# Seven products of quarters for the gate and up blocks of a two-block layer

## The chip, the cores and the metric

The kernel runs on one core of one Trainium2 chip. The metric is device microseconds of one execution. Before the change three executions took 1948.46, 1948.71 and 1949.76 us; the median is 1948.71 us. One further execution was profiled: 1947.45 us, of which the span from its first to its last instruction is 1945.6 us.

## The reference, cut to what matters

The program computes two transformer blocks in float32 on 512 tokens of width 1024 (the second block puts 16 meta tokens in front). The change touches the two feed-forward layers of the second block:

```python
def swiglu(u, w_gate, w_up, w_down):
    return (jax.nn.silu(u @ w_gate) * (u @ w_up)) @ w_down
...
h = h + 0.5 * swiglu(rmsnorm_2(h, ffn1_norm[l]), ffn1_w_gate[l], ffn1_w_up[l], ffn1_w_down[l])
h = h + hybrid_mixer(...)
h = h + 0.5 * swiglu(rmsnorm_2(h, ffn2_norm[l]), ffn2_w_gate[l], ffn2_w_up[l], ffn2_w_down[l])
y = rmsnorm_2(h, final_norm)
return y[:, N_META:]
```

`w_gate` and `w_up` are 1024 x 2816, `w_down` is 2816 x 1024.

## The kernel before, in words

Activations lie transposed: 1024 features are 8 blocks (k = 0 to 7) of 128 partitions, tokens run along the free axis. The first feed-forward layer (FFN1) works on all n = 528 tokens, the second (FFN2) on n = 512. Every float32 operand is split into a high part, rounded to the matmul's type, and a low part, the rest; `mm3` (L233) makes a product as three matmuls: weights high by x high (L235), weights high by x low (L236), weights low by x high (L237). The split inputs are `xhi` and `xlo`.

A list of jobs (L1468, L1489) gives the order of the weight loads. `_dma` (L179) issues one from SyncE's queue into a raw tile `wraw` of which there are two. `_conv` (L186) converts four k blocks at a time, called a chunk here: ScalarE copies the raw weights to `whi` (L198), VectorE subtracts to get `wlo` (L199), each 128x512. There are five buffers of each, so a chunk is converted when the product that used the chunk five before it has ended. `w` (L219) hands the converted weights to a product.

`ffn` (L896) runs twice over one half of the 22 blocks of 128 columns of gate and up, and then the down product of that half. For each of the 11 blocks f of a half it makes the gate product (8 k blocks, three matmuls each; in FFN1 each in two parts of 264 columns, in FFN2 in one of 512), multiplies it by the row of inverse norms `r` (L933, VectorE), applies SiLU (L934, ScalarE), makes the up product, multiplies by `r` (L939) and by g (L940), and splits the result into `ahi` (L941, ScalarE) and `alo` (L942, VectorE). One gate block and the up block of the same f are called a pair below; there are 22 in each layer. The down product adds half of its result to the running `hT` (L952). In the last layer the last two down blocks are made in halves of 256 tokens (L963, L965), with the final norm behind each half (L311 to L1462).

No order is written out by hand below the code's own: the tile framework orders each engine's instructions when the program is built, and sets the waits between engines.

Of the kernel before, what the change touches and what calls it, by code (L numbers as in the profile page):

```python
# [17 lines left out]
KB = 8  # L18
# [3 lines left out]
XW = 576  # L22
EPS = 1e-6
# [143 lines left out]
class Net:  # L167
# [5 lines left out]
    def jobs(self, jobs):  # L173
        self.joblist = jobs
        self.j_dma = self.j_conv = self.k_conv = self.j_use = self.n_conv = self.n_use = 0
        self.raws, self.convd = {}, {}
        self.kept = 0

    def _dma(self, j):  # L179
        src, i, k0, nk = self.joblist[j]  # L180
        ncol = src.shape[3]
        t = self.wpool.tile([128, nk, ncol], F32, name="wraw", tag="wraw", bufs=self.RAWB)
        self.nc.sync.dma_start(t, src[i, :, k0:k0 + nk, :])
        self.raws[j] = t

    def _conv(self):  # L186

        j, k = self.j_conv, self.k_conv
        raw = self.raws[j]
        nk, ncol = raw.shape[1:]  # L190
        n = min(self.CK, nk - k)
        if j < len(self.joblist) - self.kept:
            pool, x, b = self.wpool, "w", self.CONVB
        else:
            pool, x, b = self.kpool, "k", 2 * self.kept
        hi, lo = (pool.tile([128, n, ncol], F32R, name=x + y, tag=x + y, bufs=b) for y in ("hi", "lo"))
        x = raw[:, k:k + n, :]
        self.nc.scalar.copy(hi, x)  # L198
        self.nc.vector.tensor_sub(lo, x, hi.bitcast(F32))  # L199
        his, los = self.convd.setdefault(j, ([], []))  # L200
        his += [hi[:, i, :] for i in range(n)]
        los += [lo[:, i, :] for i in range(n)]
        self.n_conv += 1
        self.k_conv += n
        if self.k_conv == nk:
            self.raws.pop(j)
            self.j_conv, self.k_conv = j + 1, 0
# [19 lines left out]

    def convert(self, free=0):

        while self.j_conv < len(self.joblist) and self.n_conv < self.n_use + free + self.CONVB:  # L230
            self._conv()

    def mm3(self, ps, whi, wlo, xhi, xlo, start, stop):  # L233
        mm = self.nc.tensor.matmul
        mm(ps, whi, xhi, start=start, stop=False)  # L235
        mm(ps, whi, xlo, start=False, stop=False)  # L236
        mm(ps, wlo, xhi, start=False, stop=stop)  # L237
# [658 lines left out]
    def ffn(self, t0, done, split=KB, half_done=None):  # L896

        nc, tc = self.nc, self.tc  # L900
        V, A, P = nc.vector, nc.scalar, nc.tensor
        n = T - t0
        parts = [(0, 264), (264, n - 264)] if n > 512 else [(0, n)]
        aw = n if n <= 512 else XW
        self.open_psum()
        with tc.tile_pool(name="ff", bufs=1) as pool:
# [7 lines left out]
            def product(p, hi, lo, x, k0, k1, first, last):  # L914
                for k in range(k0, k1):
                    for c, w in parts:
                        self.mm3(p[:, c:c + w], hi[k - k0], lo[k - k0], *x(k, c, c + w),
                                 first and k == k0, last and k == k1 - 1)

            xs = lambda k, u, v: self.x(k, t0 + u, t0 + v)  # L920
            pool.tile([128, 40 if n > 512 else 64], F32, name="pad")
            ahi = pool.tile([128, 11, aw], F32R, name="ahi")
            alo = pool.tile([128, 11, aw], F32R, name="alo")
            as_ = lambda k, u, v: (ahi[:, k, u:v], alo[:, k, u:v])
            for half in range(2):
                for f in range(11):
# [3 lines left out]
                    if half == 0 and f == 0:  # L930
                        self.rstd([self.psc() for _ in range(2 if n > 512 else 1)], t0)
                    g = pool.tile([128, n], F32, name="g", tag="g", bufs=2)
# [5 lines left out]
                    u = pool.tile([128, n], F32, name="u", tag="u", bufs=2)  # L938
                    V.tensor_mul(u, p, r)  # L939
                    V.tensor_mul(u, u, g)  # L940
                    A.copy(ahi[:, f, 0:n], u)  # L941
                    V.tensor_sub(alo[:, f, 0:n], u, ahi[:, f, 0:n].bitcast(F32))  # L942
                for m in range(split if half else KB):
                    p = psum()
                    hi, lo = self.w()
                    product(p, hi, lo, as_, 0, 6, True, False)
                    hi, lo = self.w()
                    product(p, hi, lo, as_, 6, 11, False, True)
                    h = self.hT[:, m, t0:T]
                    if half and m == 0:  # L950
                        self.x0 = XW - T
                    V.scalar_tensor_tensor(h, p, 0.5, h, op0=OP.mult, op1=OP.add)  # L952
                    if half:
                        done(m, slice(t0, T))
            if split < KB:
                ws = [[x + y for x, y in zip(self.w(), self.w())] for m in range(split, KB)]
                for c in (slice(0, n // 2), slice(n // 2, n)):
                    x = slice(t0 + c.start, t0 + c.stop)
                    for m in range(split, KB):
                        hi, lo = ws[m - split]  # L960
                        p = psum()[:, 0:n // 2]
                        for k in range(11):
                            self.mm3(p, hi[k], lo[k], ahi[:, k, c], alo[:, k, c], k == 0, k == 10)  # L963
                        h = self.hT[:, m, x]
                        V.scalar_tensor_tensor(h, p, 0.5, h, op0=OP.mult, op1=OP.add)  # L965
                        done(m, x)
                    half_done(x, self.psc())

# [457 lines left out]
    def final(self, out):  # L1426
# [3 lines left out]
        with tc.tile_pool(name="fin", bufs=1) as pool:  # L1430
            hg = pool.tile([128, KB, T], F32, name="hg")
            ss, late = self.ssq, pool.tile([128, T], F32, name="sq7")
            rc = pool.tile([128, S // 2], F32, name="rcol")
            pool.tile([128, 24], F32, name="padk")
            self.kept, self.kpool = 4, pool

            def done(m, x):
                h = self.hT[:, m, x]
                if m == 0:
# [8 lines left out]
                A.activation(hg[:, m, x], h, AF.Copy, scale=self.gain[4][:, m:m + 1])  # L1448

            def half_done(x, p):  # L1450
                p = p[:, 0:S // 2]
                self.inv_rms([p], S // 2, [ss[:, x], late[:, x]], D)
                A.copy(rc, p)
                for m in range(KB):
                    o = hg[:, m, x]
# [4 lines left out]
                    if m % 2 == 0 or m == KB - 1:  # L1460
                        k = max(m - 1, 0) if m % 2 == 0 else m
                        (nc.scalar if m % 4 == 2 else nc.sync).dma_start(  # L1462
                            out[:, k:m + 1, x.start - NM:x.stop - NM], hg[:, k:m + 1, x])
# [25 lines left out]
def ffn_jobs(a, n):  # L1489
    j = []  # L1490
    for half in range(2):
        for f in range(11 * half, 11 * half + 11):
            j += [(a[n + "_gate"], f, 0, KB), (a[n + "_up"], f, 0, KB)]
# [31 lines left out]
```

## Time and profile before

| what | value |
|---|---|
| median of three executions | 1948.71 us |
| profiled execution | 1947.45 us |
| its span, first to last instruction | 1945.6 us |
| TensorE busy in matmuls | 1925.6 us, 99% of the span |
| VectorE busy | 1141.6 us, 59% |
| ScalarE busy | 796.4 us, 41% |
| GpSimd busy | 10.3 us, 1% |
| mean granted TensorE clock | 0.998 of full speed |
| bytes moved by DMA | 171.63 MB, 88 GB/s |

Times are microseconds unless marked ns. PE is TensorE with its matmuls, PEld its weight loads, DVE VectorE, ACT ScalarE, POOL GpSimd, SP SyncE. `L235` is line 235 of the kernel. Matmuls overlap one another, so how fast they go is read from the distance of their starts, not from their durations.

### The profile page before, as it was taken

To read this page: it belongs to the slowest core of one execution; us is meant where nothing else is said; L and a number is where in the kernel's file an instruction comes from. 1 tells how busy PE (TensorE), PEld (TensorE's weight loads), DVE (VectorE), ACT (ScalarE), POOL (GpSimd) and SP (SyncE) were. 2 spreads that over 40 slices of the span, in tenths; PEclk is the share of its full clock that TensorE was granted. 3 is DMA by queue.
4 is the path that set the end of the run, shared out by engine and by line. 5 is a ranking of instruction groups with operands and counts; after the bars stand their busy time and mean duration, and the time that the engine had idled before them with its cause. 6 is when DMAs were issued, how large, how long until landed. Compare 5 with 4: busy or idle time off the path is not lost.

```text
span 1945.6 us, 29528 instructions
## 1 busy us (share of the span) xinstructions
PE 1925.6 (99%) x11682; PEld 1691.6 (87%) x11682; DVE 1141.6 (59%) x2272; ACT 796.4 (41%) x1516; POOL 10.3 (1%) x31
## 2 busy tenths in 40 slices
PE   8999999999999999999999999999999999999998
PEld 6877788999999998889898898988888888888887
DVE  6789675444344458897554645877744554434443
ACT  7456654332233344453434333444433343323333
POOL 0010000000000000000000000000000000000000
PEclk9999999999999999999999999999999999999999
DMA  4352112222322242212122213111122222233223
GB/s 155 100 151 72 45 65 94 83 95 74 104 95 87 79 131 85 74 65 94 66 98 71 87 60 104 66 66 64 59 94 94 97 92 98 82 103 109 98 80 95
DMA packets 60682, 171.63 MB, mean 88 GB/s; under 512 B 10592, under 2 KB 13120, under 8 KB 60544
## 3 DMA queue, kind: packets, MB, share of 16 engines
q1 hardware_dynamic: 59456, 168.70, 26.3%
q8 instruction: 92, 1.51, 0.3%
q10 hardware_dynamic: 1088, 1.05, 0.2%
q14 instruction: 46, 0.38, 0.1%
HBM read 167.05 MB, written 2.67 MB: 87 GB/s over the span
## 4 chain that ended last, share of the span: by engine, by line
PE 93%; DVE 4%; ACT 1%; DMA 1%; issue 1%; SPq 0%; DVEq 0%; ACTq 0%
PE pm L235 27%; PE pm L236 27%; PE pm L237 27%; PE sc L235 2%; PE sc L236 1%; PE sc L237 1%; DVE rot L1036 1%; PE pf L752 1%; DVE wlo L199 1%; PE pn L784 0%; PE so L1301 0%; PE sc L1147 0%; DMA slot<-rd 0%; PE st L1131 0%; PE pd L472 0%
## 5 line engine op out<-in xcount | busy, mean ns | idle before, releaser
L235 PE MATMUL pm<-xhi,whi 128*128 128x264 f32 (+2 forms) x2360 | 787.6, 334 | 1.1 <-DVE hT L875 0.9
L236 PE MATMUL pm<-xlo,whi 128*128 128x264 f32 (+2 forms) x2360 | 781.5, 331 | 0.0
L237 PE MATMUL pm<-xhi,wlo 128*128 128x264 f32 (+2 forms) x2360 | 779.1, 330 | 0.0
L198 ACT CAST whi<-wraw 128x512 fp32r<-128x512 f32 (+1 forms) x628 | 372.2, 593 | 813.8 <-PE pm L236 758.3
L199 DVE TENSOR_TENSOR wlo<-wraw,whi 128x512 fp32r<-128x512 f32 (+1 forms) x628 | 409.8, 653 | 314.7 <-ACT whi L198 304.0
L235 PEld LDWEIGHTS pm<-xhi,whi 128*128 128x128 f32 (+1 forms) x2360 | 444.0, 188 | 46.3 <-issue 6.9
L237 PEld LDWEIGHTS pm<-xhi,wlo 128*128 128x128 f32 (+1 forms) x2360 | 444.2, 188 | 40.8 <-issue 1.7
L236 PEld LDWEIGHTS pm<-xlo,whi 128*128 128x128 f32 (+1 forms) x2360 | 443.6, 188 | 38.8 <-issue 1.2
L236 PE MATMUL pm<-alo,whi 128*128 128x264 f32 (+1 forms) x506 | 160.4, 317 | 0.0
L235 PE MATMUL pm<-ahi,whi 128*128 128x264 f32 (+1 forms) x506 | 159.6, 315 | 0.0
L237 PE MATMUL pm<-ahi,wlo 128*128 128x264 f32 (+1 forms) x506 | 159.6, 315 | 0.0
L237 PEld LDWEIGHTS pm<-ahi,wlo 128*128 128x128 f32 x506 | 95.4, 189 | 6.0
L235 PEld LDWEIGHTS pm<-ahi,whi 128*128 128x128 f32 x506 | 95.1, 188 | 6.0
L236 PEld LDWEIGHTS pm<-alo,whi 128*128 128x128 f32 x506 | 94.9, 187 | 6.0
L933 DVE TENSOR_TENSOR g<-pm,rT 128x528 f32<-128x528 f32 (+1 forms) x44 | 30.8, 700 | 73.7 <-PE pm L237 68.5
L939 DVE TENSOR_TENSOR u<-pm,rT 128x528 f32<-128x528 f32 (+1 forms) x44 | 30.8, 700 | 72.5 <-PE pm L237 72.5
L941 ACT CAST ahi<-u 128x528 fp32r<-128x528 f32 (+1 forms) x44 | 27.6, 627 | 63.9 <-DVE u L940 63.9
L235 PE MATMUL pm<-yhi,whi 128*128 128x512 f32 x128 | 49.8, 389 | 0.0
L236 PE MATMUL pm<-ylo,whi 128*128 128x512 f32 x128 | 49.8, 389 | 0.0
L237 PE MATMUL pm<-yhi,wlo 128*128 128x512 f32 x128 | 49.8, 389 | 0.0
L942 DVE TENSOR_TENSOR alo<-u,ahi 128x528 fp32r<-128x528 f32 (+1 forms) x44 | 30.8, 701 | 30.5 <-ACT ahi L941 30.5
L1036 DVE TENSOR_TENSOR rot<-pm,rope 32x384 f32<-32x384 f32 (+3 forms) x50 | 32.5, 650 | 0.7
(414 smaller groups left out, 2268.4 us busy)
## 6 DMA issues: line engine op xcount, KB each, us to landing
wraw<-in_w_in SPq DMA_DIRECT2D x124, 512.0 KB, 3.2
wraw<-in_ffn_gate SPq DMA_DIRECT2D x44, 512.0 KB, 3.2
wraw<-in_ffn_up SPq DMA_DIRECT2D x44, 512.0 KB, 3.2
wraw<-in_ffn_down SPq DMA_DIRECT2D x32, 384.0 KB, 3.0
wraw<-in_ffn_down SPq DMA_DIRECT2D x32, 320.0 KB, 2.8
wraw<-in_w_ret_out SPq DMA_DIRECT2D x32, 256.0 KB, 2.4
slot<-rd SPq DMA_DIRECT2D x4, 1024.0 KB, 9.4
wraw<-in_w_out SPq DMA_DIRECT2D x8, 512.0 KB, 3.2
```

The costliest lines, as they stand in the source:

```text
L198: self.nc.scalar.copy(hi, x)
L199: self.nc.vector.tensor_sub(lo, x, hi.bitcast(F32))
L235: mm(ps, whi, xhi, start=start, stop=False)
L236: mm(ps, whi, xlo, start=False, stop=False)
L237: mm(ps, wlo, xhi, start=False, stop=stop)
L752: P.matmul(p[:, 0:n], q[part, n - 128:n], dk[h][part, 0:n], start=True, stop=True)
L933: V.tensor_mul(g, p, r)
L939: V.tensor_mul(u, p, r)
L941: A.copy(ahi[:, f, 0:n], u)
L942: V.tensor_sub(alo[:, f, 0:n], u, ahi[:, f, 0:n].bitcast(F32))
L1036: V.tensor_mul(tmp[o:o + half], p[i:i + half], tab[i:i + half, 1, t:T])
```

## The change

The first four pairs of each layer stay as they were. The other 18 (36 of the 44 in all) are made by Strassen's scheme (Winograd's form of it): with the input cut into quarters by k (0 to 3, 4 to 7) and by tokens (first and second half, h = 264 or 256), and the weights into gate and up by k, seven products of quarters take the place of eight. Each product has 4 k blocks of three matmuls on h columns. Four combinations of the inputs' quarters (`thi`, `tlo`) are made once in a layer, by the generator `sums`, which is advanced between the products of the plain pairs. Four sums of weights are needed in each pair: `s1` (up, both halves of k) and `s3` (up and gate, first half) by loading one operand and then adding the other with a transfer that accumulates, issued from GpSimd's queue; `s2`, twice, by additions on VectorE. Seven chunks are converted in a pair in place of four. The partial results pass through PSUM: `px` and `py` go on accumulating after ScalarE has copied an intermediate state out of them (`c1`, `c5`, `c2`). The multiplication of up by `r` moves behind the down product (`rh`, 0.5 times r), which takes two VectorE instructions in place of one. In the last layer, the output tile and the kept weights move into tiles of the feed-forward pool.

The diff, cut to its core:

```diff
+PLAIN = 4
+    def _dma_pair(self, ga, ua, i):
+        nc = self.nc
+        lo, hi = slice(0, 4), slice(4, 8)
+        g, s, u = (self.fpool.tile([128, 8, 128], F32, name=x, tag="f4", bufs=6) for x in ("fg", "fs", "fu"))
+        s1, s3, u2, s2 = s[:, lo, :], s[:, hi, :], u[:, lo, :], u[:, hi, :]
+        nc.sync.dma_start(s1, ua[i, :, lo, :])
+        nc.sync.dma_start(g, ga[i])
+        nc.sync.dma_start(s3, ua[i, :, lo, :])
+        nc.sync.dma_start(u2, ua[i, :, hi, :])
+        nc.gpsimd.dma_start(s1, ua[i, :, hi, :], accum_op=OP.add)
+        nc.gpsimd.dma_start(s3, ga[i, :, lo, :], accum_op=OP.add)
+        return g, u2, s1, s3, s2
     def _conv(self):
+        if self.joblist[j][0] == "pair":
+            g, u2, s1, s3, s2 = raw
+            V = self.nc.vector
+            if k == 2:
+                V.tensor_add(s2, s1, g[:, 0:4, :])
+            elif k == 5:
+                V.tensor_add(s2, s2, g[:, 4:8, :])
+            x = (g[:, 0:4, :], s1, s2, g[:, 4:8, :], s3, s2, u2)[k]
+            self.chunkq.append(self._split(j, x))
...
     def prefetch(self, most=None):
-        while self.j_dma < min(n, self.j_conv + self.RAWB):
+        while self.j_dma < n:
+            if self.joblist[self.j_dma][0] == "pair":
+                if self.fpool is None or self.f_dma - self.f_done >= 2:
+                    return
+            elif self.p_dma - self.p_done >= self.RAWB:
+                return
+    def wq(self, last=False):
+        self.prefetch()
+        self.convert()
+        self.n_use += 1
+        self.j_use += last
+        return self.chunkq.pop(0)
     def ffn(self, t0, done, split=KB, half_done=None):
+            def sums():
+                hT, gc = self.hT, self.gain[1 if t0 == 0 else 3]
+                for k in range(4):
...
+                    for y, kk in ((y1, k), (y2, k + 4)):
+                        A.activation(y, hT[:, kk, t0:T], AF.Copy, scale=gc[:, kk:kk + 1])
+                    yield 1
...
+                    V.tensor_sub(q[:, 0], b11, b12)
+                    V.tensor_sub(q[:, 2], b22, b12)
+                    yield 1
+                    V.scalar_tensor_tensor(q[:, 1], q[:, 0], -1.0, b22, op0=OP.mult, op1=OP.subtract)
+                    V.scalar_tensor_tensor(q[:, 3], q[:, 1], -1.0, b21, op0=OP.mult, op1=OP.subtract)
+                    yield 1
+                    for u in (0, 2):
+                        A.copy(thi[:, u:u + 2, k, :], q[:, u:u + 2])
+                        V.tensor_sub(tlo[:, u:u + 2, k, :], q[:, u:u + 2], thi[:, u:u + 2, k, :].bitcast(F32))
+                        yield 1
+            def pair(f):
+                pm = self.pmain()
+                px, py, pz = pm[:, 0, 0:h], pm[:, 1, 0:h], self.psc()[:, 0:h]
...
+                def seven(p, x, first=False, last=False, end=False):
+                    whi, wlo = self.wq(end)
+                    for k in range(4):
+                        self.mm3(p, whi[k], wlo[k], *x(k), first and k == 0, last and k == 3,
+                                 skip_group_check=True)
...
+                seven(px, b11, first=True)
+                A.copy(c1, px)
+                seven(py, t(0), first=True)
+                A.copy(c5, py)
+                seven(px, t(1))
+                A.copy(c2, px)
+                seven(pz, b21, first=True, last=True)
+                V.tensor_add(g[:, 0:h], pz, c1)
+                seven(px, t(2))
+                V.tensor_add(u[:, h:n], px, c5)
+                seven(py, b22, last=True)
+                V.tensor_add(g[:, h:n], py, c2)
+                V.tensor_mul(g, g, r)
+                A.activation(g, g, AF.Silu)
+                seven(px, t(3), last=True, end=True)
+                V.scalar_tensor_tensor(u[:, h:n], u[:, h:n], -1.0, g[:, h:n], op0=OP.mult, op1=OP.mult)
+                V.scalar_tensor_tensor(u[:, 0:h], px, -1.0, g[:, 0:h], op0=OP.mult, op1=OP.mult)
+                gated(f % 11, u)
...
-                    V.scalar_tensor_tensor(h, p, 0.5, h, op0=OP.mult, op1=OP.add)
+                    y = temp("u")
+                    V.tensor_mul(y, p, rh)
+                    V.tensor_add(self.hT[:, m, t0:T], self.hT[:, m, t0:T], y)
...
-                        V.scalar_tensor_tensor(h, p, 0.5, h, op0=OP.mult, op1=OP.add)
+                        y = temp("u")[:, c]
+                        V.tensor_mul(y, p, rh[:, c])
+                        V.tensor_add(self.hT[:, m, x], self.hT[:, m, x], y)
```

In a pair the seven products are called p0 to p6 below, in the order of the code, and the chunk that each of them uses chunk 0 to chunk 6.

## Rows read from the trace of the kernel before

**Rows 1.** The page: span, TensorE's and VectorE's busy time, granted clock in 40 slices.
```profile
span 1945.6 us, 29528 instructions
...
PE 1925.6 (99%) x11682; PEld 1691.6 (87%) x11682; DVE 1141.6 (59%) x2272; ACT 796.4 (41%) x1516; POOL 10.3 (1%) x31
...
PEclk9999999999999999999999999999999999999999
```
**Rows 2.** Windows of one pair (FFN1, FFN2): length, engines' busy, clock, DMA share, GB/s.
```profile
377.38:389.06 11.68, 11.68 (x98) 11.68 (x97) 5.33 (x8) 3.77 (x7) 0.00 (x0) 1.00 0.25 87
1612.54:1623.42 10.88, 10.88 (x49) 9.01 (x48) 5.19 (x8) 3.74 (x7) 0.00 (x0) 1.00 0.29 101
```
**Rows 3.** Timeline of VectorE in a pair of FFN1: start, duration, instruction, idle before.
```profile
365.70 0.71 DVE L933 TENSOR_TENSOR g<-pm,rT 128x528 f32<-128x528 f32 x1 [1.64 <-PE pm L237]
...
371.54 0.71 DVE L939 TENSOR_TENSOR u<-pm,rT 128x528 f32<-128x528 f32 x1 [1.64 <-PE pm L237]
372.17 0.68 DVE L199 TENSOR_TENSOR wlo<-wraw,whi 128x512 fp32r<-128x512 f32 x1
372.77 0.70 DVE L940 TENSOR_TENSOR u<-u,g 128x528 f32<-128x528 f32 x1
...
377.38 0.71 DVE L933 TENSOR_TENSOR g<-pm,rT 128x528 f32<-128x528 f32 x1 [1.64 <-PE pm L237]
```
**Rows 4.** Timeline of VectorE in FFN2: the same instruction in two pairs that follow one another.
```profile
1612.54 0.69 DVE L933 TENSOR_TENSOR g<-pm,rT 128x512 f32<-128x512 f32 x1 [1.55 <-PE pm L237]
...
1623.42 0.69 DVE L933 TENSOR_TENSOR g<-pm,rT 128x512 f32<-128x512 f32 x1 [1.55 <-PE pm L237]
```
**Rows 5.** Timeline of TensorE at the end of FFN2: the first and the 34th 256-column matmul.
```profile
1918.34 0.28 PE L235 MATMUL pm<-ahi,khi 128*128 128x256 f32 x1
...
1922.29 0.28 PE L235 MATMUL pm<-ahi,khi 128*128 128x256 f32 x1
```
**Rows 6.** Groups of VectorE by line and form, FFN1: busy, mean ns of one, idle before.
```profile
L199 DVE TENSOR_TENSOR wlo<-wraw,whi 128x512 fp32r<-128x512 f32 x120 | 82.5, 687 | 77.4 <-ACT whi L198 75.1 <-PE pm L236 2.2
...
L940 DVE TENSOR_TENSOR u<-u,g 128x528 f32<-128x528 f32 x22 | 15.4, 701 | 0.0
```
**Rows 7.** The same for VectorE in FFN2: the 256-column forms.
```profile
L1459 DVE TENSOR_TENSOR hg<-hg,sc 128x256 f32<-128x256 f32 x12 | 4.2, 416 | 2.5 <-ACT rcol L1453 2.5
...
L965 DVE SCALAR_TENSOR_TENSOR hT<-pm,hT 128x256 f32<-128x256 f32 x4 | 1.7, 424 | 5.8 <-PE pm L237 5.8
```
**Rows 8.** The same for ScalarE in FFN1.
```profile
L198 ACT CAST whi<-wraw 128x512 fp32r<-128x512 f32 x121 | 75.2, 622 | 169.7 <-PE pm L236 167.4 <-DMA wraw<-in_ffn_down 1.6 <-ACT g L934 0.3
L934 ACT ACTIVATE g<-g 128x528 f32<-128x528 f32 x22 | 14.2, 648 | 4.2 <-DVE g L933 4.2
L941 ACT CAST ahi<-u 128x528 fp32r<-128x528 f32 x22 | 13.9, 633 | 31.1 <-DVE u L940 31.1
...
L289 ACT ACTIVATE xhi<-hT,par 128x528 fp32r<-128x528 f32 x8 | 5.9, 737 | 1.7 <-DVE hT L952 1.4 <-DVE hT L875 0.3
...
L325 ACT COPY rT<-sc 128x264 f32<-128x264 f32 x2 | 0.8, 380 | 2.1 <-PE sc L317 2.1
```
**Rows 9.** Timeline of ScalarE in the pair of rows 3.
```profile
365.62 0.62 ACT L198 CAST whi<-wraw 128x512 fp32r<-128x512 f32 x1 [2.29 <-PE pm L236]
366.44 0.65 ACT L934 ACTIVATE g<-g 128x528 f32<-128x528 f32 x1 [0.20 <-DVE g L933]
```
**Rows 10.** Timeline of the tail: the last down block's sum and the square behind it.
```profile
1935.80 0.42 DVE L965 SCALAR_TENSOR_TENSOR hT<-pm,hT 128x256 f32<-128x256 f32 x1 [2.44 <-PE pm L237]
1936.25 0.42 ACT L1447 ACTIVATE sq<-hT 128x256 f32<-128x256 f32 x1 [2.95 <-DVE hT L965]
```
**Rows 11.** DMA issues: transfer, queue, count, KB each, median us from issue to landing.
```profile
wraw<-in_ffn_gate SPq DMA_DIRECT2D x44, 512.0 KB, 3.2
...
wraw<-in_w_ret_out SPq DMA_DIRECT2D x32, 256.0 KB, 2.4
...
dfmask<-in_dfmask SPq DMA_DIRECT2D x1, 256.0 KB, 6.1
```

More of the change, by code (lines that the diff above doesn't have):

```diff
@@ new lines, in _split, with keep @@
+    def _split(self, j, x):
+        n, ncol = x.shape[1:]
+        if j < len(self.joblist) - self.kept:
+            hi, lo = (self.wpool.tile([128, n, ncol], F32R, name=y, tag=y, bufs=self.CONVB) for y in ("whi", "wlo"))
+        else:
+            hi, lo = self.keep(n)
+        self.nc.scalar.copy(hi, x)
+        self.nc.vector.tensor_sub(lo, x, hi.bitcast(F32))
+        return [hi[:, i, :] for i in range(n)], [lo[:, i, :] for i in range(n)]
+    def keep(self, n):
+        if self.kslot is None:
+            k = self.fpool.tile([128, 32, 128], F32R, name="khi", tag="tlo", bufs=1)
+            self.kslot = [(k, self.fpool.tile([128, 8, 128], F32R, name="klo", tag="f4", bufs=6), 8 * i)
+                          for i in range(4)]
+            self.kfree = 0
+        if self.kfree + n > 8:
+            self.kslot.pop(0)
+            self.kfree = 0
+        k, lo, o = self.kslot[0]
+        i = self.kfree
+        self.kfree += n
+        return k[:, o + i:o + i + n, :], lo[:, i:i + n, :]
@@ L189, in _conv @@
         raw = self.raws[j]
[L190 to L193, printed above, removed]
-        else:
[L195 to L202, printed above, removed]
+        if self.joblist[j][0] == "pair":
[7 more added lines that the diff above has]
+            self.chunkq.append(self._split(j, x))
+            k += 1
+            end = 7
+        else:
+            end = raw.shape[1]
+            n = min(self.CK, end - k)
+            hi, lo = self._split(j, raw[:, k:k + n, :])
+            his, los = self.convd.setdefault(j, ([], []))
+            his += hi
+            los += lo
+            k += n
         self.n_conv += 1
-        self.k_conv += n
-        if self.k_conv == nk:
+        self.k_conv = k
+        if k == end:
             self.raws.pop(j)
+            if self.joblist[j][0] == "pair":
+                self.f_done += 1
+            else:
+                self.p_done += 1
             self.j_conv, self.k_conv = j + 1, 0
@@ L927, in ffn @@
+            made = None
+            for half in range(2):
+                for f in range(11 * half, 11 * half + 11):
+                    if f >= PLAIN:
+                        if f == PLAIN:
+                            sides.drain(made)
+                        pair(f)
+                        continue
                     hi, lo = self.w()
@@ L929, in ffn @@
                     product(p, hi, lo, xs, 0, KB, True, True)
-                    if half == 0 and f == 0:
+                    if f == 0:
                         self.rstd([self.psc() for _ in range(2 if n > 512 else 1)], t0)
-                    g = pool.tile([128, n], F32, name="g", tag="g", bufs=2)
+                        V.tensor_scalar(rh, r, 0.5, None, op0=OP.mult)
+                        made = sides.add(sums())
+                    g, u = temp("g"), temp("u")
                     V.tensor_mul(g, p, r)
@@ L937, in ffn @@
                     product(p, hi, lo, xs, 0, KB, True, True)
[L938 to L942, printed above, removed]
+                    V.tensor_mul(u, p, g)
+                    gated(f, u)
                 for m in range(split if half else KB):
@@ L1430, in final @@
         with tc.tile_pool(name="fin", bufs=1) as pool:
-            hg = pool.tile([128, KB, T], F32, name="hg")
+            hgs = []
             ss, late = self.ssq, pool.tile([128, T], F32, name="sq7")
             rc = pool.tile([128, S // 2], F32, name="rcol")
-            pool.tile([128, 24], F32, name="padk")
-            self.kept, self.kpool = 4, pool
+            self.kept = 4
             def done(m, x):
+                if not hgs:
+                    hgs.append(self.fpool.tile([128, KB, S], F32, name="hg", tag="thi", bufs=1))
                 h = self.hT[:, m, x]
+                g = hgs[0][:, m, x.start - NM:x.stop - NM]
                 if m == 0:
@@ L1447, in done @@
                     A.activation(late[:, x], h, AF.Square)
[L1448 removed]
+                A.activation(g, h, AF.Copy, scale=self.gain[4][:, m:m + 1])
             def half_done(x, p):
```

73 lines of the change are left out of this document (52 added, 21 removed).

## The prediction

> **What bounds the kernel now.** I read the page first: TensorE is busy 99% of the span, VectorE 59%, and the granted clock stands at nine tenths or more of full speed in all 40 slices [rows 1]. Busy matmuls overlap, so this alone does not say that TensorE sets the pace. The windows of one pair in each layer do: TensorE has no idle time in either, VectorE is busy for 5.33 of 11.68 us and 5.19 of 10.88 us, ScalarE for 3.77 and 3.74, GpSimd not at all, and DMA uses 25 to 29% of its share [rows 2]. The same instruction comes back after exactly one such window: 11.68 us in FFN1 [rows 3], 10.88 us in FFN2 [rows 4]. Divided by the matmuls that the code puts into a pair, 2 x 8 x 2 x 3 = 96 of 264 columns and 2 x 8 x 3 = 48 of 512, that is 121.7 ns and 226.7 ns from start to start, with nothing lost where one product follows the other. What is worth reading here is therefore the number of matmuls times their step, as long as the other engines keep up.
>
> **Part 1, the matmuls of 36 pairs.** A pair becomes 7 x 4 x 3 = 84 matmuls. In FFN1 they have 264 columns as before: 84 x 121.7 ns = 10.22 us, 1.46 less than 11.68 [rows 3]; 18 pairs give 26.3 us. In FFN2 the columns are halved, so the weights change twice as often for the same columns, and the step of 512 does not halve. The end of the kernel already has 256-column matmuls of the same kind, 33 steps in 3.95 us, 119.7 ns [rows 5]: 84 x 119.7 ns = 10.05 us, 0.83 less than 10.88 [rows 4]; 18 pairs give 14.9 us. Together 41.2 us less.
>
> Here a rule can be weighed. The rows give 119.7, 121.7 and 226.7 ns for 256, 264 and 512 columns. The Trainium skill (TensorE: Matmul & The Clock Gate, "Back-to-back issue gap") gives columns / 2.4 + 2.5 ns at the full clock, an estimate of 109, 112.5 and 216 ns; by it a pair would gain 1.35 us in FFN1 and 1.19 us in FFN2, 45.7 us in all. The rows are 9 to 11 ns longer at every width, which weighs more on the narrow matmuls, and they decide.
>
> **Part 2, VectorE and ScalarE beside them.** VectorE in a pair of FFN1: seven subtractions for `wlo` and two additions for `s2`, nine of 128x512 at 0.687 us [rows 6] = 6.2 us; three additions and two products on 264 columns at 0.42 us, by the 256-column rows [rows 7] = 2.1; two on 528 columns (g by r, `alo`) at 0.70 [rows 6] = 1.4. The sum of durations is 9.7 us. But instructions that are ready run into each other: the one at 372.17 is followed 0.60 us later though it lasts 0.68 [rows 3]. With 0.09 us of overlap on each of the 16 the engine needs 8.3 us. Either is under 10.22, and in FFN2, slightly shorter, under 10.05. ScalarE: seven copies at 0.62, SiLU 0.65, `ahi` 0.63, three copies of 264 columns out of PSUM at 0.38 [rows 8] = 6.8 us. So VectorE goes from 46% of a pair to between 81 and 97% and stays covered; I cost it at nothing. If the cover went, the price would be the waits of the rivals below.
>
> Where can TensorE be made to wait? A chunk is converted four products (5.84 us in FFN1) before its use, so weights tolerate much delay. Tighter are p2, which needs `c1` copied (one product, 1.46 us, after p0), and p6, which needs VectorE's addition from `px` after p4 (also 1.46 us). The copy takes 0.38 [rows 8], the addition 0.42 [rows 7], so each leaves about a microsecond for what stands ahead of it in its queue, and the longest single instruction there is 0.7 us.
>
> **Part 3, order.** This rests on the order in which the engines' queues are built. If it were the code's, `wlo` of the next chunk would never stand between L939 and L940, which are adjacent lines. It does: L939 at 371.54, L199 at 372.17, L940 at 372.77 [rows 3]. On ScalarE a copy for a later chunk runs at 365.62, before the SiLU at 366.44, which the code issues first [rows 9]. The built order fills gaps with what is ready.
>
> **Part 4, the transfers.** A pair loads 512 KB of gate and five times 256 KB in place of 1024 KB, so by bytes the DMA share of 0.25 becomes about 0.25 x 1.75 x 11.68 / 10.22 = 0.50 [rows 2]. SyncE's queue has four issues in place of two, two pairs ahead; the down weights behind them keep their two raw tiles. The two accumulating transfers are alone on GpSimd's queue; each waits there for the load that it adds to, the second stands behind the first, and chunks 1 and 4 wait for them. No row shows one. From below, as little as a plain 256 KB load, 2.4 us; from above, the slowest 256 KB load, 6.1 us, which queued behind others [rows 11]. A tile for `s1` becomes free during p0 of one pair and its chunk is converted at p4 of the next, eleven products or 16 us later; load and accumulation take 2.4 + 6.1 = 8.5 us even then. I take it as hidden, at nothing. The Trainium skill (DMA: Bandwidth & Descriptors, "Anatomy of one DMA") prices a transfer from GpSimd's queue at 2.0 us plus its bytes at 436 GB/s, an estimate of 2.6 us for 256 KB; by it the sum would be the same.
>
> **Part 5, the small edits.** `sums` adds per layer 4 x (4 x 0.42 + 2 x 0.70) = 12.3 us on VectorE [rows 6, 7] and 4 x (2 x 0.74 + 2 x 0.63) = 11 us on ScalarE [rows 8]. Three plain pairs leave 3 x (11.68 - 5.33) = 19 us idle on VectorE and more on ScalarE [rows 2]: nothing. If the last 6 of its 20 pieces, left to the drain before the first new pair, were done only then, 3 to 4 us a layer: 0 to 8 us. The down product's second VectorE instruction is covered by matmuls except in the last block: L965 takes 0.42 us and L1447 starts right behind it [rows 10], so one more costs 0.4 us. Moving the output and kept weights into the pool's tiles waits for products that are long done: nothing.
>
> **Sum.** 1947.45 - 26.3 - 14.9 + 0.4 = 1906.7 us against the profiled execution. It stood 1.3 us below the median of 1948.71, so on the median's scale **1908 us**, 2.1% less.
>
> **Rivals.**
>
> A. *The code's order on the queues: slower.* Place: p2 of each next pair, waiting for `c1`. From the end of p4 the code's order makes one chain through two engines: addition 0.42, `s2` 0.69, copy 0.62, `wlo` 0.69, addition 0.42, product 0.70, SiLU 0.65, copy 0.62, `wlo` 0.69, two products 0.84, `ahi` 0.63, copy 0.62, `c1` 0.38 = 8.0 us [rows 6 to 8]. TensorE has p5, p6, p0 and p1 to cover it, 4 x 12 x 121.7 ns = 5.84 us (5.75 in FFN2). Above that the chain decides: 2.15 us more a pair, 12.4 us in place of 11.68, and about 12.25 in place of 10.88. Then 18 x 0.7 + 18 x 1.4 = 37 us are lost: 1986 us. For it speaks that the slack is so small in code order; against it, rows 3 and 9 both show instructions moved ahead. Chance 0.06.
>
> B. *A partly bad order or late partner.* One VectorE instruction of 0.7 us too many ahead of the addition that p6 waits for, in each pair: 36 x 0.7 = 25 us back, 1933 us; in some pairs, anything between. For it: VectorE at 81% or more, its order fixed when the program is built. Against: a microsecond of slack at the two tight places. Chance 0.15.
>
> C. *The accumulating transfers set the pace.* It decides if the two together take longer than a pair, 5.0 us each one after the other. At 6.1 us each a pair takes 12.2 us, 36 x 2.1 = 76 us back: 1984 us. Against: they need not follow each other, and DMA has half its share free. The Trainium skill (SBUF — State Buffer, "Who interferes with whom") says that VectorE in its two-port modes keeps GpSimd from making descriptors, and names copies, casts and tensor-scalar instructions, not additions of two tensors; no run here shows either. Chance 0.05.
>
> D. *The seven products do not save time*, because going on in a bank that was just read, or changing banks, costs steps; at 10.88 / 84 = 129.5 ns a step FFN2 gains nothing, and FFN1 at 139. Against: pairs of parts in two banks show no loss now [rows 2]. The time would be near 1948. Chance 0.03.
>
> **How the numbers follow.** The forecast has the remaining 0.71, with 1904 to 1916 (the drain's 0 to 8 us, a step 0.5 ns off: 3024 x 0.5 ns = 1.5 us). A measurement can tell about 0.2%, 4 us, from no change. The range reaches from 1903 into most of B, to 1928: 0.71 plus two thirds of 0.15. Faster: the forecast, B and a little of C, 0.87; same: D and an edge of B and C, 0.03; slower: A and the rest of C, 0.10.
>
> **What would show it.** Right: the SiLU of a pair comes every 10.2 us in FFN1 pairs and 10.05 us in FFN2; PE busy without gaps there; VectorE at 8.3 us or so a pair; accumulations landing within 2.4 to 6 us; a tail 0.4 us longer. Wrong: TensorE idle before p2 released by `c1` or before p6 by VectorE (A, B), `whi` waiting for DMA (C), a longer step within a product (D).

## The result, and the profile after

The changed kernel takes **2034.22 us** (median of 4, 2029.38 to 2035.50) against 1948.59 us for the kernel before, run beside it on the same chip: a ratio of 1.0436, 95% interval 1.0417 to 1.0456. It is slower by 4.4% where 2.1% less was forecast. The profiled execution took 2029.38 us, its span 2027.6 us. (One edit of the change stands in neither the description nor the diff above: the program's `dynamic_dma_scratch_size` goes from 1024 to 4096. No run took it alone.) The page of the changed kernel, with the lines that answer to [rows 1] and the accumulating transfers, which had no row:

```profile
span 2027.6 us, 31301 instructions
...
PE 1935.2 (95%) x12114; PEld 1709.5 (84%) x12114; DVE 1313.0 (65%) x2636; ACT 897.9 (44%) x1764; POOL 73.0 (4%) x103
...
fs<-in_ffn_up SPq DMA_DIRECT2D x72, 256.0 KB, 3.1
...
fs<-in_ffn_up POOLq DMA_DIRECT2D x36, 256.0 KB, 5.2
fs<-in_ffn_gate POOLq DMA_DIRECT2D x36, 256.0 KB, 5.7
```

Span less busy time, TensorE was idle in matmuls for 92.4 us; in [rows 1] that is 20.0. Its busy time went up by 9.6 us where the sum wanted 41.2 less. So two things are to be explained: 72 us of waiting, and 51 us of matmuls that took longer. The waits of the same kernel name the first (engine, line, what it waited for: us in total, times, longest):

```profile
PE pm L306 <- DVE u L1062: 46.2, 25, 3.1
PE sc L388 <- DVE rc L385: 12.1, 3, 7.2
...
DVE fu L242 <- issue: 49.6, 22, 3.4
DVE fu L242 <- DMA fs<-in_ffn_up: 26.3, 7, 8.0
```

TensorE waits for L1062, the addition `u = px + c5` behind p4. VectorE itself waits at L242, the addition `s2 = s1 + g`, which makes weights out of an accumulated tile. In the code's order it stands directly behind L1062 of the pair ahead of its own; in the built order it is there a whole pair earlier, and in 26 of the 36 pairs directly ahead of L1062. The timelines of VectorE, TensorE and GpSimd around one such wait show how the two hang together (start, duration, instruction, idle before):

```profile
599.63 0.68 DVE L216 TENSOR_TENSOR wlo<-fs,whi 128x512 fp32r<-128x512 f32 x1
603.47 0.69 DVE L242 TENSOR_TENSOR fu<-fs,fg 128x512 f32<-128x512 f32 x1 [3.15 <-issue]
604.08 0.43 DVE L1062 TENSOR_TENSOR u<-pm,c 128x264 f32<-128x264 f32 x1
```
```profile
600.42 0.28 PE L308 MATMUL pm<-thi,wlo 128*128 128x264 f32 x1
...
601.38 0.28 PE L306 MATMUL pm<-xhi,whi 128*128 128x264 f32 x1
604.56 0.39 PE L306 MATMUL pm<-xhi,whi 128*128 128x264 f32 x1 [2.90 <-DVE u L1062]
```
```profile
596.55 0.86 POOL L204 DMA_DIRECT2D fs<-in_ffn_up  x1 [11.37 <-DVE wlo L216]
```

p4 (the `thi` matmuls) is done by about 600.7, so L1062 could start then. It starts at 604.08, right behind L242, and L242 waits from about 600.3. The accumulating transfer issued at 596.55 took 6.8 us to land, that is until about 603.4: 0.1 us before L242 starts. "Issue" as the releaser hides this; the landing time tells it. The addition that nothing needs soon stands ahead of the one that TensorE needs, in a queue that VectorE works off in order. The Trainium skill (Perfetto Trace Analysis, "Tensor Engine Instruction (MATMUL, LD_WEIGHTS)") calls the queues of ScalarE and VectorE strictly first in, first out; the trace agrees, an instruction that was ready stood for 3.4 us.

The 12.1 us at L388 are the same thing at the start of a layer. VectorE is idle for 8.04 us before the first L242, and the reciprocal that TensorE waits for stands behind it (VectorE, then TensorE):

```profile
347.50 0.69 DVE L242 TENSOR_TENSOR fu<-fs,fg 128x512 f32<-128x512 f32 x1 [8.04 <-DMA fs<-in_ffn_up]
...
350.21 0.18 DVE L385 RECIPROCAL rc<-rc 88x6 f32<-88x6 f32 x1
```
```profile
350.45 0.94 PE L388 MATMUL sc<-cst,rc 88*128 88x88 f32 x3 [7.23 <-DVE rc L385]
```

Part of the longer matmuls is the clock. Windows around the wait at 601.4 (length, busy time of PE, PEld, DVE, ACT, POOL with counts, granted clock, DMA share, GB/s):

```profile
596.00:601.40 5.40, 5.37 (x44) 5.17 (x43) 3.04 (x5) 2.87 (x7) 1.75 (x2) 1.00 0.82 202
601.40:604.50 3.10, 0.26 (x3) 0.05 (x1) 1.03 (x3) 0.00 (x0) 0.00 (x0) 1.00 0.37 70
604.50:605.80 1.30, 1.24 (x10) 1.24 (x11) 1.26 (x3) 0.00 (x0) 0.00 (x0) 1.00 0.03 6
605.90:609.30 3.40, 3.35 (x16) 3.04 (x15) 2.63 (x5) 2.06 (x4) 0.00 (x0) 0.50 0.17 48
609.30:612.60 3.30, 3.30 (x29) 3.30 (x28) 2.18 (x5) 2.13 (x4) 0.00 (x0) 1.00 0.81 242
```

After these 3 us without matmuls the granted clock fell to half (1.2 GHz), though work was there again, and in 3.4 us TensorE did 16 matmuls where it did 29 in 3.3 us at full clock. The profile of before holds no such stretch inside a feed-forward layer. Pairs come, in place of the 11.68 us of [rows 3], at these distances (timeline of ScalarE, SiLU of three pairs, 13.75 and 14.43 us apart):

```profile
580.16 0.65 ACT L1066 ACTIVATE g<-g 128x528 f32<-128x528 f32 x1 [0.36 <-DVE g L1065]
...
593.91 0.65 ACT L1066 ACTIVATE g<-g 128x528 f32<-128x528 f32 x1 [0.58 <-DVE g L1065]
...
608.34 0.64 ACT L1066 ACTIVATE g<-g 128x528 f32<-128x528 f32 x1 [0.58 <-DVE g L1065]
```

### The profile page after: what moved, and what is told of

It reads as the page before. It is cut to its first block, busy times and chain, and to the rows that moved or that the text cites. A ratio compares the mean times of both kernels' runs of the same rounds, so it can differ in the third digit from the quotient of the medians.

```text
span 2027.6 us, 31301 instructions
## 1 busy us (share of the span) xinstructions
PE 1935.2 (95%) x12114; PEld 1709.5 (84%) x12114; DVE 1313.0 (65%) x2636; ACT 897.9 (44%) x1764; POOL 73.0 (4%) x103
## 3 DMA queue, kind: packets, MB, share of 16 engines
q10 hardware_dynamic: 1088, 1.05, 0.2%
## 4 chain that ended last, share of the span: by engine, by line
PE 76%; DMA 9%; DVE 8%; issue 4%; ACT 2%; SPq 0%; POOLq 0%; DVEq 0%; ACTq 0%
PE pm L306 22%; PE pm L307 21%; PE pm L308 21%; DMA fs<-in_ffn_up 8%; PE sc L306 2%; DVE wlo L216 2%; PE sc L307 1%; PE sc L308 1%; DVE rot L1191 1%; DVE fu L242 1%; ACT whi L215 1%; PE pf L823 1%; DVE u L1062 0%; PE pn L855 0%; PE so L1456 0%
## 5 line engine op out<-in xcount | busy, mean ns | idle before, releaser
L306 PE MATMUL pm<-xhi,whi 128*128 128x264 f32 (+4 forms) x1784 | 605.9, 340 | 48.3 <-DVE u L1062 46.2
L308 PE MATMUL pm<-xhi,wlo 128*128 128x264 f32 (+4 forms) x1784 | 591.6, 332 | 4.9 <-DVE wlo L216 4.9
L307 PE MATMUL pm<-xlo,whi 128*128 128x264 f32 (+4 forms) x1784 | 592.7, 333 | 0.0
L306 PEld LDWEIGHTS pm<-xhi,whi 128*128 128x128 f32 (+1 forms) x1784 | 341.1, 191 | 93.8 <-DVE u L1062 53.2
L306 PE MATMUL pm<-thi,whi 128*128 128x264 f32 (+1 forms) x576 | 170.5, 297 | 4.3 <-DVE g L1064 2.1
L307 PE MATMUL pm<-tlo,whi 128*128 128x264 f32 (+1 forms) x576 | 164.4, 286 | 0.0
L308 PE MATMUL pm<-thi,wlo 128*128 128x264 f32 (+1 forms) x576 | 163.7, 285 | 0.0
L306 PEld LDWEIGHTS pm<-thi,whi 128*128 128x128 f32 x576 | 111.0, 193 | 11.1 <-DVE g L1064 6.0
L307 PEld LDWEIGHTS pm<-tlo,whi 128*128 128x128 f32 x576 | 111.2, 193 | 0.0
L308 PEld LDWEIGHTS pm<-thi,wlo 128*128 128x128 f32 x576 | 110.2, 192 | 0.0
```

The lines of the kernel that those rows point to most:

```text
L306: mm(ps, whi, xhi, start=start, stop=False, **kw)
L307: mm(ps, whi, xlo, start=False, stop=False, **kw)
L308: mm(ps, wlo, xhi, start=False, stop=stop, **kw)
```

## The experiments

**1. The addition back in its place.** An edge holds L242 behind what the code issues before it on VectorE, which is L1062.

```diff
-                V.tensor_add(s2, s1, g[:, 0:4, :])
+                self.tc.keep_in_program_order(V.tensor_add(s2, s1, g[:, 0:4, :]))
```

> The first addition of s2 in each pair is kept behind the VectorE instruction that the code has before it (an order edge, no wait added); nothing else changes. Theory PLACE (that addition was built a pair too early into VectorE's queue, where it waits for an accumulating transfer ahead of the additions that p6 and the norm need): TensorE's idle time falls from 84 us to under 16, the half-clock stretches inside the layers go, pairs come every 10.2 and 10.05 us, and the time is 1908 to 1918 us. Theory TRANSFERS (the accumulating transfers are too slow for a pair, wherever the addition stands): pairs stay above 11.5 us, with the copies of chunks waiting for DMA, time 1985 or more. Theory LOAD (VectorE's extra work and the starts of 84-matmul products lose the time): pairs stay above 11.5 us without any wait for DMA, time 1985 or more.

Measured: 1938.14 us, ratio 0.9944 (0.9922 to 0.9966): 96 us come back, and both waits leave the list. So the place is the greater part of the loss, and the other two theories, 1985 us or more, fall. But PLACE had 1908 to 1918 us: pairs come in turns after 10.17 and 11.71 us, not every 10.2, and about 30 us to the forecast were still open. TensorE shows nearly no idle time (busy 1911.7 of 1936.2 us). The loss shows in the starts, and in the waits of its weight loads:

```profile
PEld pm L306 <- ACT c L1056: 9.9, 36, 0.7
...
PEld pm L306 <- DVE u L1062: 4.6, 18, 0.3
```

Two places of this run, the first VectorE and TensorE, the second ScalarE and TensorE:

```profile
556.06 0.43 DVE L1062 TENSOR_TENSOR u<-pm,c 128x264 f32<-128x264 f32 x1 [1.37 <-PE pm L308]
```
```profile
556.21 0.28 PE L308 MATMUL pm<-xhi,wlo 128*128 128x264 f32 x1
556.54 0.39 PE L306 MATMUL pm<-xhi,whi 128*128 128x264 f32 x1
556.77 0.28 PE L307 MATMUL pm<-xlo,whi 128*128 128x264 f32 x1
...
561.44 0.28 PE L306 MATMUL sc<-xhi,whi 128*128 128x264 f32 x1
561.71 0.39 PE L306 MATMUL pm<-thi,whi 128*128 128x264 f32 x1
561.93 0.28 PE L307 MATMUL pm<-tlo,whi 128*128 128x264 f32 x1
```
```profile
561.27 0.38 ACT L1056 COPY c<-pm 128x264 f32<-128x264 f32 x1 [0.51 <-PE pm L308]
```

At 556.54 a product on `xhi` starts 0.05 us after L1062 ends. It is p5, which writes `py` (p0, the other product on `xhi` in `pm`, works in the tile's second buffer); L1062 reads `px`. At 561.71 p2, which writes `px`, starts 0.06 us after the copy of `py` ends. (The four matmuls into `sc` ahead of it are the start of p3: the built order of TensorE mixes products here.) Neither needs the other's bank, but `px` and `py` are two banks of one tile `pm`. In both places the first step is 0.27 to 0.33 us and the second 0.22 to 0.23, where 0.12 is the rule. No idle time is shown because the modelled end of the matmul before covers it.

**2. Only the start of each layer.** The same edge, for the first two pairs of a layer alone.

```diff
+                i2 = V.tensor_add(s2, s1, g[:, 0:4, :])
+                if self.joblist[j][3] < PLAIN + 2:
+                    self.tc.keep_in_program_order(i2)
```

> The same order edge for the first two new pairs of each layer alone; the other 32 keep the built order. PLACE: the wait of the norm's matmuls for the reciprocal at the start of each layer (12.1 us together) goes, and the half-clock stretches behind it (10.2 and 6.8 us long, half of that lost): about 20 us less, 2008 to 2018 us, while the later pairs still come every 12 to 14 us. TRANSFERS and LOAD: within 8 us of the changed kernel's 2034.

Measured: 2024.89 us, two executions of 2017.61 and 2032.17, ratio 1.0389 (1.0337 to 1.0441). The wait for the reciprocal is gone and the one for the urgent addition is there as before (47.2 us, 26 times), so the start is worth the smaller part. The median is above the 2008 to 2018 us of PLACE, and the two executions are too far apart to size the start better than to some 10 us.

**3. No accumulation.** `s1` and `s3` hold one operand only.

```diff
-        nc.gpsimd.dma_start(s1, ua[i, :, hi, :], accum_op=OP.add)
-        nc.gpsimd.dma_start(s3, ga[i, :, lo, :], accum_op=OP.add)
```

> Leaves out the two accumulating transfers, so s1 and s3 hold one operand alone. PLACE: the early additions then wait for plain loads, which land some 5 us sooner, and most of the idle time goes though they may still be built early: 1910 to 1940 us. TRANSFERS: the same. LOAD: unchanged, above 1990 us.

Measured: 1950.78 us, ratio 1.0018 (1.0007 to 1.0029). With no accumulation to wait for, 83 of the 86 us of loss go, and TensorE's wait for the urgent addition shrinks from 46.2 to 4.1 us, without the edge of run 1. It is still 11 us above the 1910 to 1940 that was expected, and 38 us above run 5 below. If the second loss, which run 5 takes away, is whole here, it is 25.5 of them; that is not shown. Nor is the order the same: the addition now stands two or four places ahead of the urgent one, where it was directly ahead of it.

**4. Plain transfers from GpSimd.** The same two transfers, without the addition.

```diff
-        nc.gpsimd.dma_start(s1, ua[i, :, hi, :], accum_op=OP.add)
-        nc.gpsimd.dma_start(s3, ga[i, :, lo, :], accum_op=OP.add)
+        nc.gpsimd.dma_start(s1, ua[i, :, hi, :])
+        nc.gpsimd.dma_start(s3, ga[i, :, lo, :])
```

> The two transfers from GpSimd's queue are plain loads of the same bytes: they overwrite s1 and s3 and do not add. If it is the adding that makes them slow, they land in about 3 us in place of 5.2 and 5.7 and the time falls toward 1940 us; if it is the queue and the traffic beside them, they still take about 5 us and the time stays above 2000 us.

Measured: 1996.48 us, ratio 1.0243 (1.0214 to 1.0273). The transfers still wait for the first load and take the same bytes, but land sooner:

```profile
fs<-in_ffn_up POOLq DMA_DIRECT2D x36, 256.0 KB, 4.1
fs<-in_ffn_gate POOLq DMA_DIRECT2D x36, 256.0 KB, 3.9
```

They land 1.1 and 1.8 us sooner than when they add, and the kernel gets 38 us back, 1.05 us a pair. The built order is the same (L242 directly ahead of the urgent addition in 26 pairs), and the gain is about what the transfer that L242 waits for lands sooner. The time lies between the two cases of the forecast: the adding is one part of the landing time, the queue and the traffic the rest.

**5. Two tiles in place of one.** Run 1, with `px` and `py` in tiles of their own.

```diff
-                pm = self.pmain()
-                px, py, pz = pm[:, 0, 0:h], pm[:, 1, 0:h], self.psc()[:, 0:h]
+                px, pz = self.pmain()[:, 0, 0:h], self.psc()[:, 0:h]
+                py = (self.pst, self.pso)[f % 2]()[:, 0:h]
```

> The run with the addition kept in place, and the two PSUM accumulators of a pair as two tiles instead of the two banks of one. Theory: what is left of the loss, 0.72 us a pair, comes from the one tile: the third product is held until ScalarE has copied the other bank, the sixth until VectorE has read the other bank. With two tiles a pair comes every 10.2 us in FFN1 and 10.05 us in FFN2, 36 x 0.72 = 26 us less: 1912 us (1907 to 1918). Rival: VectorE and ScalarE are too full, so that converted weights come just in time; then nothing changes, 1934 to 1942 us. Second rival: going on in a bank costs steps at each change of product, also 1934 to 1942 us.

Measured: **1912.67 us**, ratio 0.9811 (0.9795 to 0.9828), in the middle of what was expected; both rivals (late weights, changes of bank) fall. The SiLU of three pairs in FFN1 and two in FFN2, then windows of one pair of FFN1 and of 9.90 us, just short of a pair, in FFN2:

```profile
565.89 0.64 ACT L1066 ACTIVATE g<-g 128x528 f32<-128x528 f32 x1
...
576.10 0.64 ACT L1066 ACTIVATE g<-g 128x528 f32<-128x528 f32 x1
...
586.29 0.64 ACT L1066 ACTIVATE g<-g 128x528 f32<-128x528 f32 x1
```
```profile
1608.10 0.63 ACT L1066 ACTIVATE g<-g 128x512 f32<-128x512 f32 x1
...
1618.07 0.63 ACT L1066 ACTIVATE g<-g 128x512 f32<-128x512 f32 x1
```
```profile
565.90:576.10 10.20, 10.20 (x86) 10.20 (x86) 9.02 (x17) 6.26 (x14) 1.73 (x2) 1.00 0.81 187
1618.10:1628.00 9.90, 9.90 (x86) 9.90 (x85) 8.83 (x17) 6.13 (x13) 1.77 (x2) 1.00 0.73 174
```

A pair takes 10.20 us in FFN1 and 9.97 in FFN2; the forecast was 10.22 and 10.05. One thing more has changed: the built order of TensorE no longer mixes products, each stands whole with its 12 matmuls. The late starts right behind the two copies speak for the shared tile, but this run doesn't part the tile from the order that came with it.

**6. Two tiles, the addition left where it was.** The diff of run 5 on the changed kernel.

> The changed kernel with two PSUM tiles in a pair, and the addition left where the built order puts it. Theory (the two losses are separate): the addition still stands ahead of urgent work and waits for an accumulating transfer, so most of the loss stays: 1995 to 2030 us. Rival (the shared tile is what turns a short wait into a long one): 1908 to 1930 us.

Measured: 2033.33 us, ratio 1.0441 (1.0425 to 1.0458), 3 us above what was expected and far from the rival. So the tiles alone give nothing that shows: while VectorE is late by microseconds, it doesn't matter which product it holds. But the addition did not stay quite where it was. The built order has L242 three places ahead of L1062 in 30 pairs (ahead of L1060), where it was directly ahead of it, so it starts to wait earlier. Its wait is here put down to the transfer by name, in 35 of 36 pairs. Which product it holds shows in the tile names:

```profile
PE pm L306 <- DVE u L1062: 74.6, 27, 4.4
...
DVE fu L242 <- DMA fs<-in_ffn_up: 119.8, 35, 6.0
```
```profile
603.67 0.39 PE L306 MATMUL pm<-thi,whi 128*128 128x264 f32 x1 [0.42 <-DVE u L1062]
```

It is now p6 (`thi`), which the prediction called tight; in the changed kernel it was p5 (`xhi`), one product earlier. The one fault hides the other: the tiles give 0.9 us without the edge, less than the spread of either kernel, and 25.5 us with it. What they give with the addition in exactly its old place, no run shows.

**7 and 8. The sums on GpSimd.** In place of the two accumulating transfers and the second load of one operand; run 7 with both repairs, run 8 with neither. (Line numbers are one lower.)

```diff
-        nc.sync.dma_start(s3, ua[i, :, lo, :])
-        nc.gpsimd.dma_start(s1, ua[i, :, hi, :], accum_op=OP.add)
-        nc.gpsimd.dma_start(s3, ga[i, :, lo, :], accum_op=OP.add)
+        nc.gpsimd.tensor_add(s3, s1, g[:, lo, :])
+        nc.gpsimd.tensor_add(s1, s1, u2)
```

> The run with both repairs, and the two sums of weights made by two additions on GpSimd from tiles already loaded, in place of two accumulating transfers and one load: 1024 KB in place of 1792 KB a pair. Theory (once nothing urgent stands behind them, the accumulating transfers are hidden): as the run with both repairs, within 4 us. Rival 1: the transfers still cost, then faster by more than 4 us. Rival 2: GpSimd beside VectorE makes VectorE's instructions longer, which is 81% busy, then slower by 5 to 40 us.

> The changed kernel with the two sums made by additions on GpSimd, nothing else changed. Here the built order puts the addition of the whole sum behind the urgent addition in most pairs. Theory (the order takes transfers as landed sooner than they land, and is right about instructions): the large waits go, and what stays is the shared tile: 1935 to 1955 us. Rival (the order is bad whatever makes the sums): 1990 to 2040 us.

Measured: 1945.93 us for run 7, ratio 1.0001 (0.9972 to 1.0029), 33 us above run 5: the second rival. The line of `s2` in run 5 and in run 7 (duration of one: least, median, most), and GpSimd's group in run 7 between 560 and 630 us:

```profile
L242 DVE TENSOR_TENSOR fu<-fs,fg x36: 679/681/684, 381.7 to 1826.5; 128x512 f32<-128x512 f32 x36
```
```profile
L241 DVE TENSOR_TENSOR fu<-fs,fg x36: 676/1477/1798, 381.6 to 1852.1; 128x512 f32<-128x512 f32 x36
...
L204 POOL TENSOR_TENSOR fs<-fs,fu 128x512 f32<-128x512 f32 x7 | 10.8, 1541 | 4.0 <-DMA fu<-in_ffn_up 3.9
```

The addition `s2`, which falls beside one on GpSimd, takes about twice its time. The Trainium skill (SBUF — State Buffer, "Who interferes with whom") says that a VectorE instruction with two SBUF inputs contends with a GpSimd instruction that reads SBUF; these rows agree. ScalarE's copies behind that sum come late: TensorE waits 13.1 us in all for `c2` (L1057). Run 8 takes 1989.20 us, ratio 1.0214 (1.0197 to 1.0231), and hit neither range. Its order is the one that the theory wanted: in 26 of 36 pairs the addition stands directly behind the urgent one. TensorE's wait for the urgent addition is 15.8 us, where the changed kernel has 46.2, and about 10 of these come from the contention: in 19 of 26 waits a subtraction beside a GpSimd addition, 1.4 to 1.8 us long in place of 0.68, stands ahead of the urgent addition, as in this timeline of VectorE:

```profile
584.16 1.43 DVE L215 TENSOR_TENSOR wlo<-fs,whi 128x512 fp32r<-128x512 f32 x1
585.52 0.42 DVE L1061 TENSOR_TENSOR u<-pm,c 128x264 f32<-128x264 f32 x1
```

The 33 us of run 7 and the 25.5 us of the shared tile on top of run 5 would make 1971 us; the other 18 are not parted. So the order is better with sums that come from an instruction, and the contention keeps this run from telling what the better order is worth.

**9 and 11. Fewer plain pairs.** Run 5 with `PLAIN` at 2 and at 1 in place of 4.

> The run with both repairs, and two plain pairs per layer in place of four: 40 pairs as seven products. Theory (a pair is now bounded by its matmuls alone): two more pairs in each layer at 1.48 and 0.91 us less, 4.8 us less: 1908 us, if the sums of the activations are ready. Rival (most of the 12 us of VectorE work for those sums is now done while TensorE waits): up to 8 us a layer back, 1910 to 1924 us.

> The run with both repairs, and one plain pair per layer: 42 pairs as seven products. Theory (matmuls alone, and the order fills the sums of activations into what VectorE has idle): 2.4 us below the run with two plain pairs, 1901 us (1899 to 1903). Rival (one plain pair of 11.68 us, 5.3 of it busy on VectorE, no longer covers 12.3 us of sums): 3 to 8 us a layer back, 1907 to 1917 us.

Measured: **1903.23 us** at 2, ratio 0.9769 (0.9753 to 0.9785), the best version of this study and faster than both kernels. It is 9.4 us below run 5 and 5.7 below run 10, which has the same number of pairs as run 5. 4.8 less than run 5 (1908 us) was expected, and nothing shows of the rival's up to 8 us a layer, so the sums of activations are still hidden. At 1 it is 1923.35 us, ratio 0.9866 (0.9847 to 0.9886): 20 us back, more than either theory had. The sums of activations are not the reason: TensorE waits for them for less than 3 us in all. The timelines of ScalarE and of TensorE in the run with one plain pair, at the start of FFN2:

```profile
1561.30 0.62 ACT L215 CAST whi<-fs 128x512 fp32r<-128x512 f32 x1 [6.22 <-DMA fs<-in_ffn_up]
```
```profile
1563.76 2.08 PE L388 MATMUL sc<-cst,rc 128*128 128x128 f32 x8 [5.43 <-DVE rc L385]
```

The first accumulated tile is now converted before the row of inverse norms is made. ScalarE's copy of it waits 6.22 us for the transfer. Behind the copy in ScalarE's queue stands the step of the norm (L384) whose result VectorE's reciprocal (L385) needs, and then TensorE. It is the same fault at another first reader. TensorE waits 10.8 us at L388 in this run (0.6 in run 5), and the clock falls behind the wait:

```profile
1563.70:1575.00 11.30, 11.07 (x63) 9.92 (x63) 10.12 (x22) 10.19 (x18) 0.97 (x2) 0.84 0.31 89
```

**10. Two additions done twice.** On run 5, L1060 (ahead of the urgent addition) and L242 (right behind it).

```diff
                 V.tensor_add(g[:, 0:h], pz, c1)
+                V.tensor_add(g[:, 0:h], pz, c1)
...
                 self.tc.keep_in_program_order(V.tensor_add(s2, s1, g[:, 0:4, :]))
+                self.tc.keep_in_program_order(V.tensor_add(s2, s1, g[:, 0:4, :]))
```

> The run with both repairs, and two of VectorE's additions in each pair done twice with the same result: 0.43 us ahead of the addition that the seventh product waits for, and 0.68 us right behind it. VectorE is busy for 9.0 of 10.2 us in a pair, and for 8.8 of 9.9. Theory (about a microsecond of slack before either tight place): 9.0 + 0.9 still fits, so 0 to 0.2 us a pair: 1912 to 1920 us. Rival (VectorE's order leaves no slack, what it does more shows in full): 36 x 0.9 to 36 x 1.1 = 32 to 40 us more: 1943 to 1953 us.

Measured: 1908.98 us, ratio 0.9799 (0.9784 to 0.9813): no cost. It is 3.7 us below run 5 and 3 below what was expected, but within the spread of run 5 (1908.88 to 1914.88). VectorE is busy for 9.80 of 10.20 us and TensorE still has no gap:

```profile
565.90:576.10 10.20, 10.20 (x86) 10.20 (x86) 9.80 (x19) 6.17 (x12) 1.73 (x2) 1.00 0.73 189
```

So the slack of about a microsecond at the tight places was there, for work that is ready.

## Why the prediction was wrong

**Where the 121.6 us went** (changed kernel less run 5). By the runs, in the order of the repairs: 96 for the place of one addition, 25.5 for the shared tile and the order on TensorE that came with it. The other way round they would be 0.9 and 120.7 (run 6), so the two amounts belong to their order. By the pages of the two profiles (span 2027.6 and 1913.1): 70.4 us more idle time on TensorE and 44.1 us more busy time. Of the latter, run 1 still has 20.6 us over run 5, the late starts behind the shared tile; the other 23.5 are put down to the clock, which was granted at 0.984 on average in the changed kernel and at 0.998 in run 1. That is 0.014 x 2 x 2028 = 57 us more at half clock, which can cost up to 28 us. No run changed the clock alone, so this share is argued, and the 20.6 are rough, since the profiled execution of run 5 had a mean clock of 0.994 itself.

With both repairs the sum comes out: 1912.67 us (run 5), inside the 1904 to 1916 of the forecast. What failed is that the sum took the other engines and the transfers as hidden.

**Part 1, the matmuls: right.** 10.20 us a pair for 10.22, and 9.97 for 10.05, once nothing else stood in the way (run 5). Rival D, that going on in a bank costs steps, is out. The formula weighed there is stated by the Trainium skill (TensorE: Matmul & The Clock Gate, "Back-to-back issue gap") for an isolated matmul, which the prediction left out; the rows decided.

**Part 2, VectorE's load and slack: right in size.** 9.0 us a pair within the 8.3 to 9.7 worked out, and the slack bears 1.1 us more (run 10). It was incomplete in its places. p2 and p6 were called tight for what they read and write; p2 also had to wait for the copy of `py`, and p5 for the reading of `px`, since both lie in one tile. Run 5 gave back 0.71 us a pair. p4 was not named at all, though it needs `c2` one product after p2, as p2 needs `c1`; in run 7 this is where TensorE waits.

**Part 3, order: the step that failed first.** "The built order fills gaps with what is ready" was read from [rows 3, 9], which don't show as much: the copy moved ahead in [rows 9] had itself waited 2.29 us, and in [rows 3] L940, whose operands were there at 372.25, stood behind L199 until 372.77. Nothing in them shows how the order treats an operand that comes by a chain of two transfers. The reader of such an operand was built a pair early, ahead of the urgent addition, where it was not ready. Why the order puts it there is open: that it reckons transfers as landing sooner than they do is not shown by itself. That the one instruction's place cost 96 us is (run 1).

**Part 4, the transfers: costed at nothing, and the cover was not there.** The accumulation took 5.2 and 5.7 us in the median, inside the bounds of 2.4 to 6.1, single ones up to 8.9. But the deadline was taken from the chunk of `s1` itself, 16 us away. In the built order the first reader is the addition for `s2`, a pair earlier and ahead of urgent work, which by the 10.22 us of a pair leaves some 6 of the 16 us, an estimate. The load for the wait at 617.7 was issued at 607.7 and its sum landed at 617.7: 10 us for load and accumulation, not 8.5. In its own place the same addition waits for nothing that TensorE sees. The DMA share, forecast at 0.50, was 0.73 to 0.81 in run 5, and still set no pace. Nor did the two transfers: in run 5 they took 5.7 and 6.1 us in the median, together more than a pair, and pairs came every 10.20 us, since the second does not stand behind the first (those of one pair were issued at 580.98 and 581.52). So rival C as it was put is out.

**Rival B had the place and missed the price.** It was one VectorE instruction too many ahead of the addition that p6 waits for, at 0.7 us a pair, the duration of that instruction. In an in-order queue the price is its duration plus whatever it still waits for: here 3.15 us before 0.69. With that price, and the clock on top, B would have ended on the slower side, where none of its 0.15 was put.

**Part 5: right.** The sums of activations cost nothing that shows with four plain pairs or with two (run 9). The 0.4 us of the tail came too: TensorE waits 1.31 us for the last square in run 5, 0.85 before.

## What to carry to other kernels

When a change brings an operand by a longer way (two transfers in a row, another queue), look for its first reader on every in-order engine, and ask what stands behind that reader; price the place by the wait, not by the reader's own duration. Where the order is built by a program, pin the readers of such operands behind the urgent work, and give accumulators that are read at different times tiles of their own. When the one repair gives less than the sum promised, look at steps from start to start, since a busy TensorE can hide a late product in the modelled end of the one before.

## What the hardware showed that was not expected

- A transfer of 256 KB that accumulates took 5.2 and 5.7 us from issue to landing in the median, the same transfer without the addition 4.1 and 3.9 (run 4), a plain one from SyncE's queue 3.1.
- Three microseconds without matmuls were followed, 1.3 us after work had begun again, by 3.4 us at half clock (changed kernel, 601.4 to 609.3); at the start of FFN1 7.2 us of waiting went with about 10 us at half clock.
- A late start of a product also cost its second matmul: 0.22 to 0.23 us for the second step in place of 0.12, in both places of run 1 that are shown.
- Beside two additions on GpSimd a pair, 1.3 and 1.6 us in the median, the VectorE addition took 1.48 us in the median in place of 0.68 (run 7).
